# Tree attention on one core: the order of V's loads, GpSimd's copies and the stores, and the first and last loads in other sizes

## The chip, the cores and the metric

The kernel runs on one core of one Trainium2 chip. The metric is the time of one execution on the device in microseconds (us), the median of three runs. A profile of one execution goes with it; the span that it shows is a little shorter than the time, as it begins with the first instruction of the program.

## The reference

Masked attention over 8 batches of 12 heads (96 heads), 512 positions, 64 dimensions, in fp32. The positions are the nodes of a binary tree in heap order, and a node sees itself and its ancestors only:

```python
mask = np.zeros((seq, seq))
for i in range(seq):
    mask[i, i] = 1
    parent = i
    while parent > 0:
        parent = (parent - 1) // 2
        mask[i, parent] = 1
scores = np.einsum('bhqd,bhkd->bhqk', Q, K) * scale      # scale = 1/sqrt(64)
scores = scores + (1 - mask) * (-1e9)
weights = np.exp(scores - np.max(scores, axis=-1, keepdims=True))
weights = weights / (np.sum(weights, axis=-1, keepdims=True) + 1e-10)
return np.einsum('bhqk,bhkd->bhqd', weights, V).astype(np.float32)
```

One head of Q, K, V or the output is 512 x 64 x 4 bytes, 131 KB.

## The kernel before

Heads are loaded in twelve groups of eight ("octets", o = 0 to 11), computed in 48 pairs (i = 0 to 47) and stored in 24 groups of four ("quads", q = 0 to 23). Partition p holds the four nodes 4p to 4p+3, so partitions 0 to 31 hold the nodes under 128 (the top of the tree), 32 to 63 those of level 7 and 64 to 127 the leaves. All loads go through GpSimd's DMA queue, because they cast fp32 to bf16 on the way:

```python
loads = ctx.enter_context(tc.tile_pool(name="loads", bufs=4))
vloads = ctx.enter_context(tc.tile_pool(name="vloads", bufs=4))
opool = ctx.enter_context(tc.tile_pool(name="opool", bufs=15))
NV = 4
...
def load(kept, name, pool, src, o, h0=0, n=8, rows=(0, 128)):
    if o not in kept:
        kept[o] = pool.tile([P, 8, 4, D], bf16, name=name)
    nc.gpsimd.dma_start(
        out=kept[o][rows[0]:rows[1], h0:h0 + n, :, :].rearrange("p h t d -> p h (t d)"),
        in_=src[rows[0]:rows[1], 8 * o + h0:8 * o + h0 + n, :],
    )
```

V has to be spread into the tile `vt`, from which TensorE reads it beside columns of ones. Four DMAs bring an octet of V; two of them go straight into `vt`. GpSimd copies the top rows to four places, VectorE the rest:

```python
def load_v_tiles(o):
    load_v(o, 0, 8, (64, 128))
    for half in range(2):
        nc.gpsimd.dma_start(
            out=vts[o % NV][32 * half:32 * half + 32, :, VCOL[1]:VCOL[1] + 2 * D],
            in_=Vr[32:64, 8 * o:8 * o + 8, 2 * D * half:2 * D * half + 2 * D],
        )
    load_v(o, 0, 8, (0, 32))

def spread_top(o, h0=0, h1=8):
    for j in range(4):
        nc.gpsimd.tensor_copy(
            out=vts[o % NV][32 * j:32 * j + 32, h0:h1, VTOP:VTOP + D],
            in_=vsts[o][0:32, h0:h1, UNITS[TOP + j][1], :],
        )

def spread_leaves(o, upper, h0=0, h1=8):
    nc.vector.tensor_copy(
        out=tile_pair(o, 64 if upper else 0, h0, h1, upper),
        in_=vsts[o][64:128, h0:h1, upper:3 + upper:2, :],
    )
```

The program of GpSimd, in its order. A `yield` only sets where in the program's text the next piece is put; the engine runs its own instructions one after the other:

```python
BEHIND = 8
AHEAD = 3
NO = NQ // 2                       # 12

def pool_program():
    for h0 in (0, 2):
        load_k(0, h0, 2)
        load_q(0, h0, 2)
    load_v(0, 0, 4)
    load_k(0, 4, 4)
    load_q(0, 4, 4)
    load_v(0, 4, 4)
    load_k(1, 0, 4)
    load_q(1, 0, 4)
    spread_top(0, 0, 4)
    load_v_tiles(1)
    load_k(1, 4, 4)
    load_q(1, 4, 4)
    spread_top(0, 4, 8)
    yield
    yield
    for o in range(2, NO):
        load_k(o)
        load_q(o)
        load_v_tiles(o)
        spread_top(o - 1)
        yield
        for q in (2 * o - BEHIND, 2 * o + 1 - BEHIND):
            if q >= 0:
                store(nc.gpsimd, q)
    for q in range(NQ - BEHIND, NQ - 1):
        yield
        store(nc.gpsimd, q)
        if q == NQ - BEHIND + AHEAD:
            spread_top(NO - 1)
```

The main loop; `transpose` and `evac` bring K and Q of a pair into the form for the scores, `values` multiplies by V, `norm` divides and writes the output tile `of`. The last quad goes out through the queues of SyncE and ScalarE:

```python
for i in range(NP + 1):            # NP = 48
    if i < NP:
        scores1(i)
        scores2(i)
    ...
    if i >= 1:
        values(i - 1)
        norm(i - 1)
    for n in (1 if i == 0 else i + 2,):
        if n < NP:
            transpose(n)
            evac(n)
    ...
    spread_vector(i)
    ...                            # the next piece of pool_program
    if i == NP - 1:
        store(nc.sync, NQ - 1, 0, 2)
store(nc.sync, NQ - 1, 2, 1)
store(nc.scalar, NQ - 1, 3, 1)
```

In the profile, line 183 is `load`, 201 the two DMAs straight into `vt`, 209 `spread_top`, 223 `spread_leaves`, 259 `transpose`, 285 `evac`, 346 `values`, 375 the last step of `norm` and 383 `store`.

Of the kernel before, what the change touches and what calls it, by code (L numbers as in the profile page):

```python
# [34 lines left out]
VCOL = (164, 32, 230, 96)  # L35
# [72 lines left out]
def kernel(  # L108
# [7 lines left out]
    nc = tc.nc  # L116
    B, H, S, D = Q.shape
# [3 lines left out]
    NQ = B * H // 4  # L121
# [9 lines left out]
    Vr = V.rearrange("b h (p t) d -> p (b h) (t d)", t=4)  # L131
# [31 lines left out]
    NV = 4  # L163
    NE = 3
    vts, e2s = [], []
# [13 lines left out]
# [9 lines that stand above are left out]
    def load_k(o, h0=0, n=8):  # L188
        load(ksts, "kst", loads, Kr, o, h0, n)

    def load_q(o, h0=0, n=8):
        load(qsts, "qst", loads, Qr, o, h0, n)

    def load_v(o, *args):
        load(vsts, "vst", vloads, Vr, o, *args)

    def load_v_tiles(o):

        load_v(o, 0, 8, (64, 128))
        for half in range(2):  # L200
            nc.gpsimd.dma_start(  # L201
                out=vts[o % NV][32 * half:32 * half + 32, :, VCOL[1]:VCOL[1] + 2 * D],
                in_=Vr[32:64, 8 * o:8 * o + 8, 2 * D * half:2 * D * half + 2 * D],
            )
        load_v(o, 0, 8, (0, 32))

    def spread_top(o, h0=0, h1=8):
        for j in range(4):
            nc.gpsimd.tensor_copy(  # L209
                out=vts[o % NV][32 * j:32 * j + 32, h0:h1, VTOP:VTOP + D],  # L210
                in_=vsts[o][0:32, h0:h1, UNITS[TOP + j][1], :],
            )

    def tile_pair(o, p, h0, h1, first):

        c, step = VCOL[first], VCOL[first + 2] - VCOL[first]
        return vts[o % NV][p:p + 64, h0:h1, c:c + 2 * step].rearrange(
            "p h (t d) -> p h t d", t=2
        )[:, :, :, 0:D]
# [8 lines that stand above are left out]
    def swapped(src, step):  # L228

        return bass.AP(  # L230
            src.tensor, src.offset, [list(src.ap[0]), list(src.ap[1]), [step, 2], [1, D]]
        )

    def spread_l7(o):

        nc.vector.tensor_copy(  # L236
            out=tile_pair(o, 64, 0, 8, 0),
            in_=swapped(vts[o % NV][0:64, :, VCOL[3]:VCOL[3] + D], -D),
        )

    def spread_l7_natural(o, quad, h0, h1):
# [140 lines left out]
    def store(eng, q, h0=0, n=4):  # L382
        eng.dma_start(  # L383
            out=Or[:, 4 * q + h0:4 * q + h0 + n, :],
            in_=ofs[q][:, h0:h0 + n, :, :].rearrange("p h t d -> p h (t d)"),
        )


    BEHIND = 8

    AHEAD = 3
    NO = NQ // 2

    def pool_program():

        for h0 in (0, 2):
            load_k(0, h0, 2)
            load_q(0, h0, 2)
        load_v(0, 0, 4)
        load_k(0, 4, 4)  # L400
        load_q(0, 4, 4)
        load_v(0, 4, 4)
        load_k(1, 0, 4)
        load_q(1, 0, 4)
        spread_top(0, 0, 4)
        load_v_tiles(1)
        load_k(1, 4, 4)
        load_q(1, 4, 4)
        spread_top(0, 4, 8)
        yield  # L410
        yield
        for o in range(2, NO):
            load_k(o)
            load_q(o)
            load_v_tiles(o)
            spread_top(o - 1)
            yield
            for q in (2 * o - BEHIND, 2 * o + 1 - BEHIND):
                if q >= 0:
                    store(nc.gpsimd, q)  # L420
        for q in range(NQ - BEHIND, NQ - 1):
            yield
            store(nc.gpsimd, q)
            if q == NQ - BEHIND + AHEAD:
                spread_top(NO - 1)

    def spread_first(quad, parts):

        for part in parts:
            if part < 4:  # L430
                spread_l7_natural(0, part, 4 * quad, 4 * quad + 4)
            else:
                spread_leaves(0, part - 4, 4 * quad, 4 * quad + 4)

    def spread_vector(i):

        if i == 1 or i == 2:
            spread_first(1, range(3) if i == 1 else range(3, 6))
        o, step = divmod(i + 2, 4)
        if 1 <= o < NO:  # L440
            if step == 0:
                spread_leaves(o, 0)
            elif step == 1:
                spread_leaves(o, 1)
                spread_l7(o)

    def pool_until(done, wanted):
        while done < wanted:
            next(program, None)
            done += 1  # L450
        return done

    program = pool_program()
    steps = pool_until(0, 1)
    transpose(0)
    evac(0)
    for i in range(NP + 1):
# [3 lines that stand above are left out]
        if i == 1:  # L461
            transpose(2)
            evac(2)
            spread_first(0, range(4, 6))
# [7 lines that stand above are left out]
        if i == 0:  # L472
            spread_first(0, range(4))
        spread_vector(i)
        if steps < NO:
            steps = pool_until(steps, min((i + 11) // 4, NO))
        else:
            steps = pool_until(steps, min(steps + 2, NO + (i - 2) // 2 - (NQ - 1 - BEHIND)))
        if i == NP - 1:
            store(nc.sync, NQ - 1, 0, 2)  # L480
# [32 lines left out]
```

The softmax here doesn't subtract the row's maximum and nothing guards it: scores larger than these inputs give would overflow.

## Time and profile before

| | us |
|---|---|
| time, median of 3 runs (lowest, highest) | 140.59 (140.56, 141.06) |
| span in the profile | 138.3 |
| PE (TensorE matmul) busy | 107.7 |
| GpSimd busy | 102.1 |
| VectorE busy | 96.5 |
| ScalarE busy | 84.3 |
| HBM read, written | 38.21 MB, 12.58 MB |

Busy time says how long an engine had an instruction in work, not whether anything waited for it. The strips of the page cut the span into 40 slices of 3.46 us, one digit a slice, in tenths. A line of a timeline gives start, length, engine, line of the kernel, operation, what it writes and reads, how often, and in brackets the idle time before it and what ended it. A DMA that GpSimd issues has two times: the issue, which occupies GpSimd, and the landing, some us later, when its bytes are there.

### The profile page before, as it was taken

Reading aid. Unit: us, or ns where it says so; the run is one execution under the profiler, and the core shown is the slowest. Engines: PE = TensorE matmul, PEld = TensorE weight load, DVE = VectorE, ACT = ScalarE, POOL = GpSimd, SP = SyncE. Lnnn points to the kernel's source line nnn. Section 1 sums busy time; section 2 is a strip of 40 time slices with the busy share of each in tenths; the row PEclk is TensorE's granted clock in tenths of the full one; section 3 lists DMA queues with packets and bytes.
Section 4 is the critical chain, followed back from the end, with each engine's and each line's share of the span. In section 5 each row is a group of like instructions: output and inputs, shape, how many; then the busy total and the mean of one; then the engine's idle time right before and its main releaser. Section 6 shows DMA issues by size and latency. Waiting matters only on the chain.

```text
span 138.3 us, 5482 instructions
## 1 busy us (share of the span) xinstructions
PE 107.7 (78%) x2400; PEld 78.6 (57%) x2400; DVE 96.5 (70%) x205; ACT 84.3 (61%) x98; POOL 102.1 (74%) x155
## 2 busy tenths in 40 slices
PE   0486798799879996968998995795895894997920
PEld 0243566577656774746676674574574583675610
DVE  4036688889788698759698884684784775788550
ACT  4044075768775866848686774595595486486810
POOL 6969999749599896797598399489489489489200
PEclk9999689999999999999999999999999999999985
DMA  4999999999999999999999999999999999999982
GB/s 137 155 136 189 195 192 197 198 191 198 192 198 194 335 220 195 323 227 197 295 254 196 280 272 194 257 291 198 244 303 198 229 315 202 221 366 390 364 302 92
DMA packets 44936, 32.27 MB, mean 233 GB/s; under 512 B 7280, under 2 KB 41840, under 8 KB 44912
## 3 DMA queue, kind: packets, MB, share of 16 engines
q0 software_dynamic: 44208, 30.94, 127.2%
q1 hardware_dynamic: 560, 0.85, 1.8%
q8 instruction: 18, 0.29, 0.8%
q10 hardware_dynamic: 144, 0.13, 0.3%
q14 instruction: 6, 0.05, 0.1%
HBM read 38.21 MB, written 12.58 MB: 367 GB/s over the span
## 4 chain that ended last, share of the span: by engine, by line
PE 34%; DMA 27%; DVE 16%; POOL 9%; issue 9%; ACT 1%; POOLq 0%; ACTq 0%
DMA qst<-in_Q_dram 27%; PE ob L346 15%; PE kqp L259 8%; DVE of L375 5%; PE s L296 4%; POOL vt L209 3%; DVE vt L223 3%; DVE kq L285 3%; PE s L301 3%; DVE vt L236 3%; PE s L325 3%; PE s L318 2%; DVE rec L372 2%; POOL kst L183 2%; POOL out_dram L383 1%
## 5 line engine op out<-in xcount | busy, mean ns | idle before, releaser
L307 ACT ACTIVATE e<-s 128x1024 bf16<-128x1024 f32 x48 | 49.1, 1023 | 46.8 <-PE s L301 46.1
L346 PE MATMUL ob<-vt,e 128*128 128x65 bf16 (+1 forms) x960 | 39.3, 198 | 14.3 <-POOL vt L209 7.1
L346 PEld LDWEIGHTS <-e 128*128 128x128 bf16 (+1 forms) x960 | 31.3, 103 | 20.8 <-issue 9.3
L285 DVE COPY kq<-kqp 128x1024 bf16<-128x1024 bf16 x48 | 32.8, 683 | 9.5 <-PE kqp L259 9.4
L331 ACT ACTIVATE e<-s 128x768 bf16<-128x768 f32 x48 | 38.6, 805 | 0.0
L375 DVE TENSOR_TENSOR of<-ob,rec 128x512 f32<-128x512 f32 x48 | 33.2, 692 | 1.9 <-DMA out_dram<-of 0.2
L209 POOL COPY vt<-vst 32x512 bf16<-32x512 bf16 (+1 forms) x52 | 31.1, 598 | 3.5 <-DMA vst<-in_V_dram 1.3
L372 DVE RECIPROCAL rec<-ob 128x8 f32<-128x8 f32 x48 | 9.9, 207 | 23.7 <-PE ob L346 23.2
L259 PE MATMUL kqp<-ctile,qst 128*64 128x128 bf16 x384 | 20.1, 226 | 5.3 <-DMA qst<-in_Q_dram 3.2
L259 PE MATMUL kqp<-ctile,kst 128*64 128x128 bf16 x384 | 19.7, 225 | 5.2 <-DMA kst<-in_K_dram 5.2
L183 POOL DMA_DIRECT2D qst<-in_Q_dram x15 | 12.7, 849 | 11.7 <-PE kqp L259 6.6
L383 POOL DMA_DIRECT2D out_dram<-of x23 | 17.6, 768 | 5.0 <-DVE of L375 4.7
L325 PEld LDWEIGHTS <-kq 64*128 64x128 bf16 x384 | 15.9, 97 | 7.1 <-issue 1.6
L296 PE MATMUL s<-ctile 64*128 64x512 bf16 x96 | 19.4, 400 | 0.1
L301 PE MATMUL s<-kq 64*128 64x512 bf16 x96 | 18.9, 391 | 0.5 <-DVE kq L285 0.5
L183 POOL DMA_DIRECT2D vst<-in_V_dram x24 | 16.2, 676 | 2.4 <-DMA vt<-in_V_dram 2.4
L325 PE MATMUL s<-kq 64*128 64x96 bf16 (+3 forms) x384 | 17.9, 213 | 0.1
L259 PEld LDWEIGHTS <-qst 128*64 128x64 bf16 x384 | 14.0, 114 | 5.4 <-DMA qst<-in_Q_dram 4.3
L318 PE MATMUL s<-ctile 64*128 64x384 bf16 x96 | 16.2, 334 | 0.2
L259 PEld LDWEIGHTS <-kst 128*64 128x64 bf16 x384 | 12.9, 114 | 5.4 <-DMA kst<-in_K_dram 5.2
L201 POOL DMA_DIRECT2D vt<-in_V_dram x22 | 12.7, 585 | 4.1 <-DMA qst<-in_Q_dram 2.2
L183 POOL DMA_DIRECT2D kst<-in_K_dram x15 | 13.0, 868 | 2.2 <-POOLq L497 0.8
(15 smaller groups left out, 42.3 us busy)
## 6 DMA issues: line engine op xcount, KB each, us to landing
out_dram<-of POOLq DMA_DIRECT2D x23, 512.0 KB, 8.2
kst<-in_K_dram POOLq DMA_DIRECT2D x10, 512.0 KB, 10.0
qst<-in_Q_dram POOLq DMA_DIRECT2D x10, 512.0 KB, 10.1
vst<-in_V_dram POOLq DMA_DIRECT2D x13, 256.0 KB, 10.1
vt<-in_V_dram POOLq DMA_DIRECT2D x22, 64.0 KB, 9.7
vst<-in_V_dram POOLq DMA_DIRECT2D x11, 128.0 KB, 9.7
kst<-in_K_dram POOLq DMA_DIRECT2D x3, 256.0 KB, 7.2
qst<-in_Q_dram POOLq DMA_DIRECT2D x3, 256.0 KB, 7.6
```

The costliest lines, as they stand in the source:

```text
L183: nc.gpsimd.dma_start(out=kept[o][rows[0]:rows[1], h0:h0 + n, :, :].rearrange("p h t d -> p h (t d)"), in_=src[rows[0]:rows[1], 8 * o + h0 ...
L209: nc.gpsimd.tensor_copy(out=vts[o % NV][32 * j:32 * j + 32, h0:h1, VTOP:VTOP + D], in_=vsts[o][0:32, h0:h1, UNITS[TOP + j][1], :],)
L259: nc.tensor.transpose(out=dst, in_=st[i // 4][:, 2 * (i % 4) + a, t, :], identity=perm)
L285: nc.vector.tensor_copy(out=kq[:, :, :, :].rearrange("p k (x y) c -> p k x (y c)", x=2), in_=src)
L296: nc.tensor.matmul(out=sp[:, a, :], lhsT=k1code[64 * a:64 * a + 64, :], rhs=q1code[64 * a:64 * a + 64, :], start=True, stop=False,)
L301: nc.tensor.matmul(out=sp[:, a, :], lhsT=keys(i, a, TOP), rhs=qTs[i][64 * a:64 * a + 64, :, :].rearrange("p t c -> p (t c)"), start=False, ...
L307: nc.scalar.activation(out=et[:, :, :, :].rearrange("p a t c -> p (a t c)"), in_=sp[:, :, :].rearrange("p a c -> p (a c)"), func=AF.Exp, s ...
L325: nc.tensor.matmul(out=sp[:, a, :, :].rearrange("p t c -> p (t c)")[:, lo:hi], lhsT=keys(i, a, TILE2[tile2]), rhs=qTs[i][64 * a:64 * a + 6 ...
L331: nc.scalar.activation(out=e2s[i % NE][:, :, :, 32:128].rearrange("p a t c -> p (a t) c"), in_=sp[:, :, :, 32:128].rearrange("p a t c -> p ...
L346: nc.tensor.matmul(out=ob[lo:hi, a, start_o:start_o + 65], lhsT=e[:, a, QPOS[t], lo:hi], rhs=vt[:, 2 * (i % 4) + a, col:col + 65], **flags,)
L375: nc.vector.tensor_tensor(out=ofs[q][:, 2 * r:2 * r + 2, :, :], in0=vals, in1=rec[:, :, :, :].to_broadcast([P, 2, 4, D]), op=ALU.mult,)
L383: eng.dma_start(out=Or[:, 4 * q + h0:4 * q + h0 + n, :], in_=ofs[q][:, h0:h0 + n, :, :].rearrange("p h t d -> p h (t d)"),)
```

## The change

Four things at once. (1) V's nodes under 128 are loaded first of V's four DMAs, not last, and GpSimd's copies of the octet before stand between the loads of Q and V, not behind V's. This is to have the copies done sooner after their rows have landed. (2) Stores go ten quads behind the computation, not eight: the loads get two stores fewer ahead of them, and the end two more. (3) The last octet is loaded and spread in two halves of four heads, so that its first half can be used before its second has come. (4) The first K and Q come as one load of four heads each, not two of two.

```diff
-    def load_v_tiles(o):
-
-        load_v(o, 0, 8, (64, 128))
+    def load_v_tiles(o, h0=0, n=8):
+
+        load_v(o, h0, n, (0, 32))
+        load_v(o, h0, n, (64, 128))
         for half in range(2):
             nc.gpsimd.dma_start(
-                out=vts[o % NV][32 * half:32 * half + 32, :, VCOL[1]:VCOL[1] + 2 * D],
-                in_=Vr[32:64, 8 * o:8 * o + 8, 2 * D * half:2 * D * half + 2 * D],
+                out=vts[o % NV][32 * half:32 * half + 32, h0:h0 + n, VCOL[1]:VCOL[1] + 2 * D],
+                in_=Vr[32:64, 8 * o + h0:8 * o + h0 + n, 2 * D * half:2 * D * half + 2 * D],
             )
-        load_v(o, 0, 8, (0, 32))
...
-    BEHIND = 8
-
-    AHEAD = 3
+    BEHIND = 10
     NO = NQ // 2
 
     def pool_program():
 
-        for h0 in (0, 2):
-            load_k(0, h0, 2)
-            load_q(0, h0, 2)
+        load_k(0, 0, 4)
+        load_q(0, 0, 4)
         load_v(0, 0, 4)
...
+        behind = (1, 0, 8)
         for o in range(2, NO):
-            load_k(o)
-            load_q(o)
-            load_v_tiles(o)
-            spread_top(o - 1)
+            for h0, n in ((0, 8),) if o < NO - 1 else ((0, 4), (4, 4)):
+                load_k(o, h0, n)
+                load_q(o, h0, n)
+                spread_top(nc.gpsimd, *behind)
+                load_v_tiles(o, h0, n)
+                behind = (o, h0, h0 + n)
             yield
             for q in (2 * o - BEHIND, 2 * o + 1 - BEHIND):
                 if q >= 0:
                     store(nc.gpsimd, q)
+        spread_top(nc.gpsimd, *behind)
         for q in range(NQ - BEHIND, NQ - 1):
             yield
             store(nc.gpsimd, q)
-            if q == NQ - BEHIND + AHEAD:
-                spread_top(NO - 1)
...
-        if 1 <= o < NO:
+        if 1 <= o < NO - 1:
             if step == 0:
                 spread_leaves(o, 0)
             elif step == 1:
                 spread_leaves(o, 1)
                 spread_l7(o)
+        elif i + 1 in (4 * NO - 4, 4 * NO - 2):
+
+            h0 = i + 5 - 4 * NO
+            spread_leaves(NO - 1, 0, 2 * h0, 2 * h0 + 4)
+            spread_leaves(NO - 1, 1, 2 * h0, 2 * h0 + 4)
+            spread_l7(NO - 1, 2 * h0, 2 * h0 + 4)
```

(`spread_l7` and `spread_top` take the range of heads as arguments for it, and `spread_top` the engine, which is GpSimd everywhere.)

More of the change, by code (lines that the diff above doesn't have):

```diff
@@ L195, in load_v, with spread_top @@
         load(vsts, "vst", vloads, Vr, o, *args)
-    def load_v_tiles(o):
-        load_v(o, 0, 8, (64, 128))
+    def load_v_tiles(o, h0=0, n=8):
+        load_v(o, h0, n, (0, 32))
+        load_v(o, h0, n, (64, 128))
         for half in range(2):
             nc.gpsimd.dma_start(
-                out=vts[o % NV][32 * half:32 * half + 32, :, VCOL[1]:VCOL[1] + 2 * D],
-                in_=Vr[32:64, 8 * o:8 * o + 8, 2 * D * half:2 * D * half + 2 * D],
-            )
-        load_v(o, 0, 8, (0, 32))
-    def spread_top(o, h0=0, h1=8):
+                out=vts[o % NV][32 * half:32 * half + 32, h0:h0 + n, VCOL[1]:VCOL[1] + 2 * D],
+                in_=Vr[32:64, 8 * o + h0:8 * o + h0 + n, 2 * D * half:2 * D * half + 2 * D],
+            )
+    def spread_top(eng, o, h0, h1):
         for j in range(4):
-            nc.gpsimd.tensor_copy(
+            eng.tensor_copy(
                 out=vts[o % NV][32 * j:32 * j + 32, h0:h1, VTOP:VTOP + D],
@@ L232, in swapped, with spread_l7 @@
         )
-    def spread_l7(o):
+    def spread_l7(o, h0=0, h1=8):
         nc.vector.tensor_copy(
-            out=tile_pair(o, 64, 0, 8, 0),
-            in_=swapped(vts[o % NV][0:64, :, VCOL[3]:VCOL[3] + D], -D),
+            out=tile_pair(o, 64, h0, h1, 0),
+            in_=swapped(vts[o % NV][0:64, h0:h1, VCOL[3]:VCOL[3] + D], -D),
         )
@@ L404, in pool_program @@
         load_q(1, 0, 4)
-        spread_top(0, 0, 4)
+        spread_top(nc.gpsimd, 0, 0, 4)
         load_v_tiles(1)
@@ L408, in pool_program @@
         load_q(1, 4, 4)
-        spread_top(0, 4, 8)
+        spread_top(nc.gpsimd, 0, 4, 8)
         yield
         yield
+        behind = (1, 0, 8)
         for o in range(2, NO):
-            load_k(o)
-            load_q(o)
-            load_v_tiles(o)
-            spread_top(o - 1)
+            for h0, n in ((0, 8),) if o < NO - 1 else ((0, 4), (4, 4)):
[4 more added lines that the diff above has]
+                behind = (o, h0, h0 + n)
             yield
```

## The prediction

> **What bounds the kernel now.** I read the page's strips of the span first, because the busy shares alone (PE 78%, POOL 74%, DVE 70%) name no bound.
>
> ```profile
> DMA  4999999999999999999999999999999999999982
> GB/s 137 155 136 189 195 192 197 198 191 198 192 198 194 335 220 195 323 227 197 295 254 196 280 272 194 257 291 198 244 303 198 229 315 202 221 366 390 364 302 92
> ```
>
> The DMA digit is 9 in every slice but the first and the last two. The GB/s strip must be read with the cast in mind: a load reads fp32 from HBM and writes bf16, and the page counts what was written, so 198 in a slice of loads is 396 GB/s of HBM reads; a slice of stores alone shows 390. Both are the same speed. To put a number on it I asked for sums over stretches (columns: stretch, then the engines' busy time with counts, clock, DMA share, GB/s).
>
> ```profile
> 0.00:4.00 4.00, 0.00 (x0) 0.00 (x0) 1.39 (x16) 1.49 (x2) 2.94 (x8) 1.00 0.54 141
> 4.00:8.00 4.00, 2.41 (x22) 1.19 (x24) 0.69 (x1) 0.00 (x0) 4.00 (x7) 1.00 1.21 148
> 8.00:12.00 4.00, 3.69 (x50) 2.09 (x44) 2.17 (x5) 2.59 (x3) 2.57 (x6) 1.00 1.26 155
> 12.00:16.00 4.00, 2.12 (x40) 1.75 (x42) 1.74 (x6) 0.87 (x2) 3.96 (x7) 0.83 1.45 196
> 122.00:126.00 4.00, 3.73 (x91) 2.74 (x88) 3.54 (x8) 3.31 (x5) 3.71 (x6) 1.00 1.06 397
> 130.00:132.00 2.00, 1.28 (x31) 0.98 (x29) 0.84 (x3) 1.79 (x3) 0.75 (x1) 1.00 0.84 320
> 132.00:134.00 2.00, 0.78 (x20) 0.64 (x20) 1.00 (x3) 0.00 (x0) 0.00 (x0) 1.00 0.98 360
> 134.00:136.00 2.00, 0.00 (x0) 0.00 (x0) 0.25 (x1) 0.00 (x0) 0.00 (x0) 0.52 0.65 225
> ```
>
> 122 to 126 is nothing but stores: 397 GB/s, which I take as full rate. The page gives 38.21 MB read and 12.58 MB written; 50.79 MB at 397 GB/s is 127.9 us. The span is 138.3, so all there is to win is 10.4 us, and I place it. In 0 to 4 us 564 KB were moved, of which 459 KB are the constants and 105 KB loads (210 KB of HBM): 1.7 us of work, 2.3 lost. 4 to 8 (148, so 296 of HBM): 1.0 lost. 8 to 12 (310): 0.9. From 12 on 196, full. In the tail: 130 to 132 lose 0.4, 132 to 134 0.2, 134 to 136 0.9, the last 2.3 us nearly all of themselves. With 0.2 for 126 to 130 (377 and 375 GB/s) that is 3.9. What is left, about 2.3, is spread over 100 us in the middle.
>
> Then the chain of waits, in order of time, to see whether the middle is bandwidth or latency:
>
> ```profile
> 77.88 10.59 DMA qst<-in_Q_dram
> 88.47 0.04 issue
> 88.52 0.43 PE kqp L259 x8
> ...
> 89.03 10.06 DMA qst<-in_Q_dram
> 99.10 0.04 issue
> 99.14 0.43 PE kqp L259 x8
> ...
> 99.67 9.97 DMA qst<-in_Q_dram
> ```
>
> Each Q load takes 10 us from issue to landing, is used at once, and the next one is issued 0.55 us after it landed. In the trace's semaphore records GpSimd's DMAs signal on eight semaphores in turn, so each waits for the landing of the one eight before; an octet of heads (K, Q, four of V, two stores) is eight DMAs. The loop looks like latency but is bandwidth: an octet is 24 heads of loads and 8 of stores at 131 KB, 4.19 MB, 10.57 us at 397 GB/s, and the period here is 10.6.
>
> Last, GpSimd in order of time, where the change works:
>
> ```profile
> 89.03 0.88 POOL L183 DMA_DIRECT2D qst<-in_Q_dram  x1 [1.77 <-PE kqp L259]
> 90.31 0.69 POOL L183 DMA_DIRECT2D vst<-in_V_dram  x1 [0.40 <-DMA vt<-in_V_dram]
> 90.99 1.16 POOL L201 DMA_DIRECT2D vt<-in_V_dram  x2
> 92.13 0.60 POOL L183 DMA_DIRECT2D vst<-in_V_dram  x1
> 92.77 2.67 POOL L209 COPY vt<-vst 32x512 bf16<-32x512 bf16 x4
> ```
>
> Four copies, 2.67 us, end at 95.44; PE starts the first product of that octet at 95.49. Its Q landed at 88.47, so the copies are 7 us behind it.
>
> **What the skill says.** The Trainium skill, "DMA: Bandwidth & Descriptors", section Specifications, gives about 358 GB/s as HBM's limit per core and 435 as the fabric's. This trace shows 397 for whole stretches; the measurement decides and I use 397. "Perfetto Trace Analysis", section DMA Optimizations, says both that larger DMAs fill the bandwidth better and that splitting lets work start sooner when the engines are idle. Here they are not idle before the tail, and the fixed part is visible: a 2-head load needs 3.9 us to landing (list of DMA issues: 128 KB, 3.9) for 0.66 us of bytes. "SBUF — State Buffer", on the shared port pair, says that some VectorE copies and any GpSimd work exclude each other. It agrees: the leaf copies of L223 take 0.42 us at 69.86 and 0.81 at 71.93, beside the GpSimd copies.
>
> **The change, part by part.**
>
> Start: before, four issues of two heads (K, Q, K, Q, 0.72 us apart) go ahead of V, each 0.66 us of bytes, so GpSimd hands out work a little slower than it is moved. After, two issues of four heads (about 0.8 us each, like the four-head ones that follow) hand out 1.32 us of bytes each. I take 0.3 us of the 1.0 lost in 4 to 8. The 0.9 lost in 8 to 12 stays: all ten first loads had been issued by 8.7 and the rate was still 155, so issue is not its cause. The first transposes start about 1 us later, which is hidden: values of pair 0 wait until 13 us for the second half of Q anyway.
>
> Copies between Q and V: with V's top 32 rows first, they land 0.66 us after Q, and the copies run from 0.55+0.88 = 1.4 to 4.1 us after Q instead of to 7.0. PE's first product then waits for its own chain: from the octet's first transposes (68.08) to its first product (74.60) it is 6.5 us. So the octet gains about 0.5 to 0.9 us of lag, off the path. The new V loads go out 2.7 us later, at 4.1 us after Q; what is still queued then (rest of V, two stores, K, Q) lasts to 10.6 us after Q, so DMA does not run dry. Worth: 0.
>
> Stores ten behind: the same bytes. Two stores of 524 KB, 2.64 us, move from before the last load to after it. The last load landed at 123.0; now near 120.3. Twelve stores instead of ten follow, 15.8 us. By itself 0, but compute finishes earlier against DMA.
>
> Last heads by fours: before, compute set the end. The last copies wait in GpSimd's order behind stores, run from 123.66 to 126.42, then four pairs of products to 133.3, the last output at 134.25, and the last two stores, issued at 134.3, land 3 us later. After, the last Q lands near 119; 6.5 us to product 46 and 2.1 to product 47, with 1 us for the output: near 129. The stores last to 136. Compute leaves the path, and of the 1.5 us lost from 130 to 136 I give back 1.0.
>
> The price: GpSimd runs in order and the last octet has twelve small loads instead of six. From the landing of Q of octet 10: Q11a out at 0.55 (0.81 us), four copies (2.65), four V DMAs (2.35), K and Q (1.62): GpSimd reaches the copies of 11a at 7.98. Their V rows land at 8.3 (V10 2.65, two stores 2.65, K and Q 2.65, 0.33). Copies of four heads took 1.69 us (at 10.03), so the next V load goes out at 10.0. From issue to the first bytes I take the issue's length plus 1.07 us (first load: issued 1.27 to 2.09, its first packet in the trace at 3.18). The queued work ends at 11.9; the four small V DMAs, issued 0.57 to 0.62 us apart, hold 1.32 us of bytes and end at 13.6; the next store, out at 12.3, can move at 14.2: idle 0.3 + 0.6. Then the last copies (1.7 us) hold up the third store: idle 0.55. Sum 1.45; some lies under the engines that lag, so 1.2.
>
> Sum: -0.3 (start) -1.0 (old tail) +1.2 (new gap near 120) = -0.1 us. The timed 140.59 becomes about **140.5 us**.
>
> **The rivals.** (1) The gap does not appear, because the bytes start sooner after the issue than I take: then -1.3, 139.3. For it: the only cold measurement of that delay is the first load. (2) The gap is paid in full and the twelve stores at the end also suffer from engines that finish unevenly (128 to 130 shows 375 with GpSimd idle and stores queued): +0.5 to +1.3, 141.1 to 141.9. (3) Earlier V tops shorten every octet, because PE waits 7.1 us in total for L209: some 5 us, 135. Against it: DMA shows 9 throughout, and an octet already takes its byte time. (4) Late V loads starve DMA in each octet: 7 octets of about 1 us, 147; against it stand the 6 us still queued.
>
> **Range and chances.** Terms of -1.3 and +1.3 around a sum near 0 give 139.2 to 142.0 for 8 in 10. Two per cent is 2.8 us: faster needs nearly all the lost time of start and tail, slower needs two new gaps. Faster 0.05, same 0.89, slower 0.06.
>
> **What would show it.** Right: DMA digits of 9 up to 115 us; PE's wait for L209 nearly gone; last products before 130; a dip in GB/s near 118 to 122; stores at 390 to the end. Wrong: octets of Q loads much off 10.6 us, or no dip and an end before 136.5 in the span.

## The result, and the profile after

| | before | changed |
|---|---|---|
| time, median | 140.81 us | 144.75 us |
| lowest to highest of the runs | 140.56 to 141.06 | 144.5 to 145.55 |
| span in the profile | 138.3 us | 142.5 us |

The ratio is 1.029, 95% interval 1.024 to 1.034: slower by some 2.9%, above the range of 139.2 to 142.0. (The first line has four runs of each kernel.)

First the strips of the page, of the changed kernel:

```profile
DMA  4999999999999999999999999999999999999991
GB/s 132 150 187 196 192 196 198 194 195 197 193 197 191 199 209 333 204 205 332 198 209 334 200 212 326 203 213 325 202 216 324 169 168 212 305 312 324 338 326 43
```

The digit strip says nothing new: 9 almost to the end. The GB/s strip does. The third and fourth slices are better than before (187 and 196 against 136 and 189). From 110 to 118 us there are two slices of 169 and 168, and then the stores alone run at 305 to 338, where the kernel before had 366, 390 and 364.

Sums over stretches put numbers on it (columns: stretch and length, busy time and count of PE, PEld, DVE, ACT, POOL, clock, DMA share, GB/s). The changed kernel:

```profile
4.00:8.00 4.00, 0.64 (x9) 0.40 (x10) 0.00 (x0) 0.00 (x0) 3.37 (x5) 1.00 1.32 170
8.00:12.00 4.00, 3.75 (x40) 2.10 (x40) 0.93 (x2) 1.72 (x2) 2.36 (x6) 1.00 1.41 189
112.00:116.00 4.00, 3.72 (x84) 2.74 (x85) 3.71 (x7) 2.60 (x4) 3.43 (x8) 1.00 1.31 162
116.00:120.00 4.00, 4.00 (x100) 3.05 (x99) 2.99 (x6) 3.32 (x5) 3.96 (x8) 1.00 1.21 166
124.00:128.00 4.00, 3.49 (x76) 2.52 (x78) 3.45 (x10) 2.98 (x5) 3.61 (x5) 1.00 0.97 305
132.00:136.00 4.00, 0.00 (x0) 0.00 (x0) 0.62 (x1) 0.00 (x0) 0.00 (x0) 0.50 1.01 341
```

The kernel before, in three of these stretches:

```profile
112.00:116.00 4.00, 3.13 (x72) 2.23 (x67) 3.63 (x7) 3.32 (x5) 3.87 (x7) 1.00 1.31 258
116.00:120.00 4.00, 3.07 (x78) 2.34 (x77) 1.71 (x4) 1.86 (x3) 3.03 (x5) 1.00 1.49 199
124.00:128.00 4.00, 3.26 (x83) 2.48 (x81) 3.44 (x7) 2.86 (x4) 3.74 (x6) 1.00 1.00 387
```

Before, 124 to 128 was 387 GB/s at a DMA share of 1.00. Here it is 305 at 0.97, and 341 at 1.01 from 132 to 136, when compute is over and GpSimd's stores have long been issued. So from 124 to 136 us the DMA engines are not idle: they are busy and move less. The packets say the same. A store packet of 4 KB took 165 ns (median) from 123 to 132 us before, and 187 to 198 ns (medians of stretches of 2 us) from 120 to 138 us in the changed kernel.

The whole difference, as time lost against 397 GB/s (bytes of the trace's packets in each stretch, without the fetches of instructions, a load counted at its fp32 size; good to about 0.1), up to the last packet:

```
us lost in          before   changed   difference
0 to 12               4.27      3.50     -0.8
12 to 112             2.16      2.41     +0.25
112 to 120            0.09      1.94     +1.85
120 to last packet    2.50      4.18     +1.7
sum                   9.02     12.03     +3.0
```

The last packet ends at 136.96 before and 139.96 after, 3.0 us later. The remaining 1.2 us of the span lie behind it. A drain stands at the end of GpSimd's program; in the trace it ends at 137.31 before, 1.3 us behind GpSimd's last landing (136.03), and at 141.69 after, 1.6 us behind it (140.13). Before, this was hidden behind the stores of SyncE and ScalarE, the last of which landed at 137.34; now GpSimd's last store is the last to land but for one (140.35).

GpSimd in order of time, changed kernel, where the middle rows of the table come from:

```profile
107.01 0.75 POOL L183 DMA_DIRECT2D qst<-in_Q_dram  x1 [2.13 <-DMA qst<-in_Q_dram]
107.81 2.55 POOL L209 COPY vt<-vst 32x512 bf16<-32x512 bf16 x4
110.31 1.17 POOL L183 DMA_DIRECT2D vst<-in_V_dram  x2
111.46 1.10 POOL L202 DMA_DIRECT2D vt<-in_V_dram  x2
112.54 0.78 POOL L183 DMA_DIRECT2D kst<-in_K_dram  x1
113.28 0.78 POOL L183 DMA_DIRECT2D qst<-in_Q_dram  x1
114.50 1.70 POOL L209 COPY vt<-vst 32x256 bf16<-32x256 bf16 x4 [0.44 <-DMA vst<-in_V_dram]
116.15 1.17 POOL L183 DMA_DIRECT2D vst<-in_V_dram  x2
117.30 1.09 POOL L202 DMA_DIRECT2D vt<-in_V_dram  x2
118.38 1.53 POOL L383 DMA_DIRECT2D out_dram<-of  x2
119.95 1.70 POOL L209 COPY vt<-vst 32x256 bf16<-32x256 bf16 x4
121.60 6.00 POOL L383 DMA_DIRECT2D out_dram<-of  x8
```

From the issue of the Q load at 107.01 to that of the next load at 110.31 it is 3.3 us, 2.55 of them copies, and there are two such pauses more (113.28 to 116.15, 119.14 to 121.60). After 121.60 the stores are issued 0.75 us apart, far faster than they are moved: from there nothing in GpSimd's order can slow them.

One more reading is needed for what follows. A DMA is done by 16 engines, and each reports its own end to the semaphore, so the trace has 16 ends for each DMA. "First" and "last" below are the first and the last of them; what a store takes is the step from one store's end to the next one's.

```
                        issued   first end (step)   last end (step)
before,   Q of octet 11  110.21   117.09             120.24
          store of q 16  118.31   123.76 (1.29)      127.48 (1.29)
          store of q 18  122.12   126.50             131.04
          store of q 19  122.87   127.81 (1.31)      132.14 (1.10)
          store of q 20  126.37   129.69 (1.88)      133.44 (1.30)
          store of q 21  127.11   131.26 (1.57)      134.72 (1.28)
changed,  Q11, 1st half  107.01   111.13             114.11
          V top rows     110.31   112.33             114.45
          store of q 17  123.84   129.58 (1.52)      131.17 (1.64)
          store of q 18  124.58   131.13 (1.55)      132.85 (1.68)
          store of q 19  125.33   132.69 (1.56)      134.41 (1.56)
```

Before, the leading engine runs 3 us ahead of the last one at the end of the loads. In the changed kernel it is through with the Q load at 111.1, while the next load was issued only at 110.31: it has nothing to do until about 112 (an estimate: the first end of V's top rows, less 0.33 us for their bytes). By the second half of Q the engines lie 1.1 us apart (117.50 and 118.62), and the leading one then takes 1.5 to 1.7 us for nearly every store, where 1.3 was usual.

### The profile page after: what moved, and what is told of

The parts are those of the page before. It is cut to its first block, busy times and chain, and to the rows that moved or that the text cites. A ratio compares the mean times of both kernels' runs of the same rounds, so it can differ in the third digit from the quotient of the medians.

```text
span 142.5 us, 5490 instructions
## 1 busy us (share of the span) xinstructions
PE 108.2 (76%) x2400; PEld 79.5 (56%) x2400; DVE 95.9 (67%) x208; ACT 84.4 (59%) x98; POOL 104.0 (73%) x163
## 4 chain that ended last, share of the span: by engine, by line
DMA 27%; PE 25%; POOL 24%; issue 9%; DVE 7%; POOLq 0%
DMA vst<-in_V_dram 13%; POOL vt L209 11%; PE ob L346 10%; DMA vt<-in_V_dram 7%; DMA qst<-in_Q_dram 7%; PE kqp L259 5%; PE s L296 3%; POOL vst L183 3%; POOL vt L202 3%; DVE of L375 3%; POOL qst L183 3%; POOL kst L183 3%; PE s L301 2%; PE s L325 2%; PE s L318 2%
## 5 line engine op out<-in xcount | busy, mean ns | idle before, releaser
L346 PE MATMUL ob<-vt,e 128*128 128x65 bf16 (+1 forms) x960 | 40.2, 199 | 9.6 <-DVE of L375 4.4
L259 PE MATMUL kqp<-ctile,qst 128*64 128x128 bf16 x384 | 20.6, 227 | 4.2 <-issue 3.5
L259 PEld LDWEIGHTS <-qst 128*64 128x64 bf16 x384 | 14.6, 115 | 4.1 <-issue 3.2
L183 POOL DMA_DIRECT2D vst<-in_V_dram x26 | 16.7, 648 | 0.0
L202 POOL DMA_DIRECT2D vt<-in_V_dram x24 | 14.0, 591 | 0.0
```

Source lines behind the costliest of these rows:

```text
L183: nc.gpsimd.dma_start(out=kept[o][rows[0]:rows[1], h0:h0 + n, :, :].rearrange("p h t d -> p h (t d)"), in_=src[rows[0]:rows[1], 8 * o + h0 ...
L259: nc.tensor.transpose(out=dst, in_=st[i // 4][:, 2 * (i % 4) + a, t, :], identity=perm)
L346: nc.tensor.matmul(out=ob[lo:hi, a, start_o:start_o + 65], lhsT=e[:, a, QPOS[t], lo:hi], rhs=vt[:, 2 * (i % 4) + a, col:col + 65], **flags,)
```

## The experiments

Each run stands beside runs of the kernel before on the same chip; ratios are to those, with 95% intervals. The results first:

| run | what it is | us | ratio |
|---|---|---|---|
| changed | all four parts | 144.75 | 1.029 (1.024 to 1.034) |
| e1_whole | changed, last octet whole | 142.55 | 1.014 (1.004 to 1.025) |
| e3_before_behind10 | before, stores ten behind | 140.99 | 1.002 (0.999 to 1.005) |
| e4_skew | changed, uneven loads ahead of the last stores | 146.58 | 1.043 (1.035 to 1.051) |
| e5_sync | before, stores held until the last V has landed | 150.14 | 1.064 (1.054 to 1.074) |
| e6_level_not_dry | e5_sync and a load ahead of the stores | 149.95 | 1.065 (1.058 to 1.073) |
| e10_load_among | e5_sync and a load among the stores | 152.2 | 1.081 (1.071 to 1.090) |
| e9_fours_late | changed, last copies moved back | 142.52 | 1.015 (1.012 to 1.018) |
| e7_whole_late | changed, last octet whole, last copies moved back | 139.13 | 0.988 (0.981 to 0.995) |
| e8_before_first4 | before, first K and Q by fours | 138.94 | 0.988 (0.979 to 0.997) |
| e11_whole_late8 | e7_whole_late, stores eight behind | 139.78 | 0.996 (0.993 to 0.999) |

**Which theory of the long store steps.** Three stood at first: that engines at the same point slow each other (LEVEL), that a long run of stores is slow by itself (TWELVE), and that only the pauses count (GAP).

*e1_whole*, the last octet as the others:

```diff
-            for h0, n in ((0, 8),) if o < NO - 1 else ((0, 4), (4, 4)):
+            for h0, n in ((0, 8),):
```

> The changed kernel with the last octet loaded and spread whole, as the other octets are (no loads by fours at the end); all else as changed. Three theories for the slow end of the changed kernel (stores of 512 KB land 1.55 to 1.6 us apart from 122 us on, against 1.3 before). LEVEL: the gaps between the small last loads let all 16 DMA engines come level (from the first to the last engine's completion of one DMA 1.1 us there, 3.7 us before), and level engines store more slowly. Without the small loads there is no gap, the engines keep their spread of about 3 us, twelve stores land 1.3 us apart: 139.5 to 140.5 us. TWELVE: a long run of stores with no loads between is slow by itself; twelve stores still land about 1.6 us apart: 143 to 144 us. GAP: only the idle time of the small loads counts, about 2 us of it: 142.5 us, with stores unchanged at 1.6 us apart.

Measured 142.55, the number that GAP gave, but not for its reason. The small loads are gone, and the trace shows a pause all the same, and a longer one: GpSimd's last copies now stand behind only two stores and wait for V's top rows.

```profile
113.22 1.55 POOL L383 DMA_DIRECT2D out_dram<-of  x2
118.56 2.54 POOL L209 COPY vt<-vst 32x512 bf16<-32x512 bf16 x4 [3.80 <-DMA vst<-in_V_dram]
121.05 5.97 POOL L383 DMA_DIRECT2D out_dram<-of  x8
```

The two stores ahead of the copies took 1.30 us (first and last engine alike); those behind took the leading engine 1.5 to 1.6 from the first one on. That was the pattern to follow.

*e3_before_behind10*, one constant of the kernel before:

```diff
-    BEHIND = 8
+    BEHIND = 10
```

> The kernel before with stores ten groups behind and nothing else changed. LEVEL: no small loads, no gap, the engines keep their spread of 3 us or more, the twelve stores at the end land 1.3 us apart, time 140 to 141 us as before. TWELVE: two more stores in the run at the end make it slower: stores about 1.5 us apart on average, 142 to 143.5 us. GAP: no gap, time as before, 140.5 to 141.

140.99, no difference: ten behind costs nothing by itself. The steps were not as any theory had them. Six of the stores took about 1.29 us. GpSimd's other five, issued behind the last copies, took the leading engine 1.5 to 1.9, while the spread of the engines was 2.6 us before the copies and still 2.1 to 2.5 behind them. TWELVE doesn't explain the jump, and LEVEL doesn't fit well.

*e4_skew* puts the engines out of step. The added loads are extra work that no output needs:

```diff
+            if o == NO - 1:
+                for n, heads in ((0, 16), (1, 32), (2, 48)):
+                    nc.gpsimd.dma_start(
+                        out=spare[4 * n:4 * n + 4, 0:heads, :], in_=Qr[4 * n:4 * n + 4, 0:heads, :],
+                    )
             yield
```

> The changed kernel with three loads added behind the last load of V, of four partitions and 16, 32 and 48 heads each, into a tile that nothing reads. Each occupies only some of the DMA engines, for about 0.65, 1.3 and 2 us, so that the engines go into the run of stores at different points. They add 393 KB, 1.0 us of the mean engine and 2 us of the most loaded. LEVEL: the stores then land about 1.3 to 1.4 us apart, packets of 4 KB take 165 to 170 ns against 190 to 206 in the changed kernel; the time falls or stays although bytes are added, 141.5 to 144.5 us. TWELVE: stores stay 1.55 to 1.6 us apart, and the added bytes make it 145.5 to 147 us. GAP: same as TWELVE.

146.58. The engines went into the stores 4.4 us apart, and still the first end went on in steps of 1.72, 1.63, 1.57 and 1.54 us, while the last end, that of the engines with the largest added load, went on in steps of 1.29, 1.28, 1.30 and 1.34. At the same time, on the same stores, some engines took long steps and some short ones. So it belongs to the single engine, not to the HBM as a whole. From 121 to 122 us, ahead of the first store, only 8 to 12 of the 16 engines had a packet under way. Read with the ends, the engines with long steps had come to the end of their queue by then, and those with short steps still had a load in work; the trace doesn't name the engines, so this is argued here and tested in the next runs.

*e5_sync* makes all engines run empty in the kernel before:

```diff
             spread_top(o - 1)
+            if o == NO - 1:
+                spread_top(NO - 1)
             yield
...
-            if q == NQ - BEHIND + AHEAD:
-                spread_top(NO - 1)
```

> The kernel before with GpSimd's last four copies moved ahead of the stores of the last octet, so that no store goes out until the last of V has landed: the DMA engines run dry for some 4 us and start level into ten stores. Nothing of the last octet is loaded in small pieces. LEVEL: the ten stores land about 1.6 us apart, 3 us more than 1.3 apart, and the time is 140.6 + 4 + 3, 147 to 148.5 us. TWELVE and GAP: the idle time alone is added and the stores land 1.3 us apart as before, 144 to 145.5 us.

150.14, more than expected, as the pause was longer (the queue is empty from 124 to 128). The long steps came out: nine stores, no step of the leading engine under 1.52 us, without a small load anywhere. LEVEL and an after-effect of an empty queue (DRY) both explain it; the next run parts them.

*e6_level_not_dry*, e5_sync with one added load, into a tile that nothing reads:

```diff
             if o == NO - 1:
                 spread_top(NO - 1)
+                nc.gpsimd.dma_start(out=spare[:, :, :], in_=Qr[:, 0:8, :])
             yield
```

> The kernel of the run e5_sync (no store until the last of V has landed) with one more load of eight heads behind the wait and ahead of the stores, into a tile that nothing reads. The DMA engines start level into that load, but have it in work (2.65 us) when the first store reaches them, so none of them stands idle between the last load and the first store. LEVEL (engines at the same point store slowly): stores still land 1.55 us apart; 150.1 + 2.65, about 152.5 to 153.5 us. DRY (an engine whose queue runs empty ahead of the stores moves them slowly from then on, one that goes over from loads without a pause moves them at full rate): stores land 1.3 us apart, packets of 4 KB take 165 ns instead of 190; 149.5 to 150.5 us in spite of the added load.

149.95 us: a megabyte more to read, and the same time within the spread of the runs (the spans of the two profiles are 146.9 and 148.5). The engines were level (0.8 us from first to last), and the first stores took 1.28, 1.29 and 1.30 us. The stretch of stores, first in e5_sync, then in e6_level_not_dry:

```profile
130.00:134.00 4.00, 2.69 (x62) 1.94 (x56) 1.80 (x4) 2.61 (x4) 3.36 (x5) 1.00 1.00 313
134.00:138.00 4.00, 0.10 (x6) 0.00 (x0) 0.90 (x2) 0.00 (x0) 0.00 (x0) 0.89 1.01 328
```

```profile
134.00:138.00 4.00, 0.78 (x20) 0.64 (x20) 1.11 (x3) 0.00 (x0) 1.49 (x2) 0.78 1.03 408
138.00:142.00 4.00, 0.00 (x0) 0.00 (x0) 0.00 (x0) 0.00 (x0) 0.00 (x0) 0.50 1.02 371
142.00:146.00 4.00, 0.00 (x0) 0.00 (x0) 0.00 (x0) 0.00 (x0) 0.00 (x0) 0.50 1.03 371
```

The share is 1.0 in both; the rate is 313 to 328 against 408. LEVEL falls: level engines can store at full rate. For the first stores it counts whether an engine meets them with an empty queue or coming from a load.

That is one way into the long steps and not the only one. From 138 on the rate in e6_level_not_dry is 371, and from 144 to 146 the median packet of 4 KB takes 189 ns. GpSimd had issued seven stores by 133.0, and no engine stood idle from 134 to 145 (16 packets under way throughout). SyncE's store came in at 138, but e10_load_among, below, has SyncE's stores too and keeps its rate. In e3_before_behind10 as well the share of 4-KB packets of up to 170 ns falls from 0.55 (127 to 129 us) to 0.15 (132 to 134), again with about 16 packets under way. What ends the full rate there is not shown.

*e10_load_among* asks what ends the long steps (`spare` is again a tile that nothing reads):

```diff
             store(nc.gpsimd, q)
+            if q == NQ - BEHIND + 1:
+                nc.gpsimd.dma_start(out=spare[:, :, :], in_=Qr[:, 0:8, :])
```

> The kernel of the run e5_sync (DMA engines empty for some 4 us, then stores, which land 1.55 us apart) with one load of eight heads into an unread tile behind the fourth of the stores. DRY, with a state that a load ends: the stores ahead of the load land 1.55 us apart, those behind it 1.3; about 151 us (150.1 + 2.65 - 6 x 0.27). DRY, with a state that lasts until the end whatever comes: 1.55 on both sides, 152.8 us. A limit of stores in a row without loads, whatever went before: 1.3 just behind the load, rising later.

152.2 lies between the expectations, since the stores of SyncE came among GpSimd's (ends from 142.2 to 146.2) and stretch the steps there. The undisturbed steps decide: 1.62 and 1.60 us ahead of the load, 1.29 and 1.29 at the end behind it. In stretches, ahead and behind:

```profile
130.00:133.00 3.00, 1.86 (x34) 1.18 (x33) 1.77 (x4) 2.40 (x3) 3.00 (x5) 1.00 1.01 317
145.00:146.00 1.00, 0.00 (x0) 0.00 (x0) 0.00 (x0) 0.00 (x0) 0.00 (x0) 0.50 1.03 399
```

A load ends them; nine stores in a row, in e5_sync, don't.

**Which part of the change.**

*e9_fours_late* keeps the small loads and moves the copies back:

```diff
-                spread_top(nc.gpsimd, *behind)
+                if h0 == 0:
+                    spread_top(nc.gpsimd, *behind)
...
-        spread_top(nc.gpsimd, *behind)
         for q in range(NQ - BEHIND, NQ - 1):
             yield
             store(nc.gpsimd, q)
+            if q == NQ - BEHIND:
+                spread_top(nc.gpsimd, NO - 1, 0, 4)
+            elif q == NQ - BEHIND + 2:
+                spread_top(nc.gpsimd, NO - 1, 4, 8)
```

> The changed kernel with the last octet still in fours, but GpSimd's last copies moved behind the loads and behind three and five of the stores, so that they no longer hold up loads. If the small loads are slow by themselves: 142 to 143 us. If only the waits of GpSimd that let the queue run empty count: 139.3 to 140.8 us, GB/s near 390 of HBM all the way to 126 us.

142.52, the number of the case in which the small loads cost by themselves. One reason is in the trace (two lines of GpSimd's timeline and one stretch):

```profile
110.58 1.17 POOL L183 DMA_DIRECT2D vst<-in_V_dram  x2
111.73 1.10 POOL L202 DMA_DIRECT2D vt<-in_V_dram  x2
112.00:116.00 4.00, 3.99 (x95) 3.02 (x96) 3.16 (x8) 2.77 (x4) 4.00 (x7) 1.00 1.16 145
```

The four V loads of half an octet take GpSimd 2.2 us to issue and hold 1.32 us of bytes (524 KB at 397 GB/s). GpSimd was busy in all of 112 to 116, with no wait, and the rate was 145 GB/s. The copies for octet 10 stood ahead of these loads still. That is not all of the cost: the first four stores took 1.36 to 1.43 us, the later ones 1.5 to 1.7, with two pauses of their own for copies (119.05 to 120.69, 122.23 to 123.87). The run doesn't part the two.

*e7_whole_late* takes both away:

```diff
-            for h0, n in ((0, 8),) if o < NO - 1 else ((0, 4), (4, 4)):
+            for h0, n in ((0, 8),):
...
-        spread_top(nc.gpsimd, *behind)
         for q in range(NQ - BEHIND, NQ - 1):
             yield
             store(nc.gpsimd, q)
+            if q == NQ - BEHIND + 1:
+                spread_top(nc.gpsimd, *behind)
```

> The run e1_whole (changed kernel, last octet whole) with GpSimd's last copies behind four of the twelve stores at the end and not behind two, so that the queue is not empty when they wait. LEVEL and DRY alike: no gap near 122 us, stores 1.3 us apart for most of the tail, and the better start (about 1.1 us) is kept: 139 to 140.3 us. If a run of twelve stores is slow by itself: 142 us as e1_whole.

139.13, 1.2% under the kernel before, with ten behind and the new order still in it. Stretches of its tail:

```profile
120.00:124.00 4.00, 4.00 (x101) 2.94 (x96) 3.32 (x8) 3.45 (x4) 4.00 (x6) 1.00 1.00 381
124.00:128.00 4.00, 3.46 (x82) 2.61 (x81) 3.34 (x8) 2.86 (x4) 0.88 (x2) 1.00 1.02 366
```

Even here the leading engine went over to long steps (first end in steps of 1.5 us from 125.4 on), but the last one kept 1.29 us to 133.6, and the last one sets the end.

*e8_before_first4*, the kernel before with the first loads alone:

```diff
-        for h0 in (0, 2):
-            load_k(0, h0, 2)
-            load_q(0, h0, 2)
+        load_k(0, 0, 4)
+        load_q(0, 0, 4)
```

> The kernel before with the first K and Q as one load of four heads each. If the start of the changed kernel (less lost by 12 us: 3.5 us of full rate against 4.3) comes from this part alone, 139.6 to 140.0 us; if it comes from the order of V's rows or is lost again, 140.5 to 141.

138.94, a little better than expected. The stretches say where:

```profile
4.00:8.00 4.00, 0.53 (x8) 0.40 (x8) 0.00 (x0) 0.00 (x0) 3.36 (x5) 1.00 1.27 167
8.00:12.00 4.00, 3.05 (x35) 1.72 (x35) 0.69 (x1) 1.12 (x2) 1.71 (x5) 1.00 1.44 194
```

8 to 12 had been 155 with loads of two heads. This part of the change is the good one. Up to 12 us it loses 3.4 us of full rate, where the kernel before lost 4.3; the span is 1.4 us shorter, so some 0.5 of the gain lies elsewhere and is not explained.

*e11_whole_late8*, e7_whole_late with `BEHIND = 8`:

> The run e7_whole_late with the stores eight groups behind, so that of the changed kernel only the order of V and the copies and the first loads by fours are left. As no engine runs empty before the last stores, 138.7 to 139.5 us, the same as e7_whole_late (139.1) and e8_before_first4 (138.9): then the number of groups behind and the order of the copies are worth nothing here and the first loads are worth all of it. If the order of V is worth something by itself: 138.0 to 138.5.

139.78, above what was expected, and 0.4% under the kernel before in 22 runs, its interval overlapping those of e7_whole_late and e8_before_first4. The order of V and the copies shows no gain of its own. The best of all runs are e8_before_first4 and e7_whole_late, not to be told apart.

## Why the prediction was wrong, point by point

**What bounds the kernel**: right. DMA is the bound, and an octet takes its byte time: the lost time from 12 to 112 us differs by 0.25 us in 100.

**Start, -0.3**: direction right, size wrong: -0.8. The step that failed is "The 0.9 lost in 8 to 12 stays". That all ten first loads had been issued by 8.7 was true, but the rate there depended on their size: with loads of four heads the same stretch lost 0.2 (189 GB/s where 155 had been). That the engines run empty between two-head loads would fit, and is only argued.

**Copies between Q and V, worth 0**: no run shows a gain or a loss from them away from the end, and PE's wait for the copies (7.1 us before) is gone from the list of waits. In its place GpSimd waits for V:

```profile
POOL vt L209 <- DMA vst<-in_V_dram: 8.2, 5, 3.4
```

That wait was not in the prediction. In the middle it cost nothing; at the end, in e1_whole, it is the pause.

**Stores ten behind, 0 by itself**: right (e3_before_behind10, 1.002).

**Compute leaves the path, -1.0**: it did leave it, though later than predicted: the last output is ready at 132.6 (near 129 in the prediction), and the last store lands at 140.3. Nothing came back, because the stores themselves became slower, and because GpSimd's own end, 1.2 us, came out from behind the stores of the other queues.

**The gap near 120, +1.2**: there, and +1.85 in the table. The step that failed is "The queued work ends at 11.9", counted from the landing of Q. A landing is the end of the last of 16 engines, and the leading one was 3 us ahead. So the gap opened earlier than worked out, already behind the copies for octet 10 (at 111.1, where 11.9 us behind Q of octet 10 is 118.3), and "some lies under the engines that lag, so 1.2" went the wrong way: the lag hides from the landing that the engines ahead have run empty. A third term erred the other way. The 1.07 us from the end of an issue to the first bytes, taken from the first load, was 0.57 in e5_sync, with all engines empty (issue over at 127.39, first packet at 127.96).

**"Stores at 390 to the end"**: this is the step that failed most, and a cost that the sum left out. The changed kernel's engines, having run empty, moved the stores at 305 to 341 GB/s, the leading one in 1.5 to 1.7 us each and not 1.3. An estimate: twelve stores at about 0.27 us more are 3.2 us, of the 4.18 lost behind 120; the tail before lost 2.50 there, in part waiting for compute, and the net is the +1.7 of the table. The rival that named uneven engines, read off 375 GB/s from 128 to 130, had the right view in hand and the wrong reading. In the kernel before, too, up to 3 of the 16 engines stood idle from 127.5 to 128 us, ahead of q 20 (step 1.88, then 1.57), and the leading one took long steps from there.

Rivals (3) and (4) of the prediction are out: the octets are neither shorter nor starved (the leading engine ends Q of octets 8, 9 and 10 at 81.99, 92.58 and 103.18, 10.6 us apart).

## What to carry to other kernels

Where DMA is the bound, count what is still queued from the leading engine's end and not from the landing, and keep work in the queue through every pause of the engine that issues, above all where loads give way to stores. Small transfers are dear where their issue takes longer than their bytes (2.2 us for 1.32 here). A change of several parts may hide a good one: here the two lines of the start were worth about 0.8 us of lost time (1.2%, with an interval of 0.3 to 2.1%, in the one run that has them alone), and the rest took it back and 2.9% on top.

## What was not expected of the hardware

A DMA engine that meets a store with an empty queue moves this store and the following ones at about 0.83 of its rate (in e5_sync some 1.56 us a store against 1.29; a 4-KB packet in 192 ns against 165), with the queue full behind it, through all of the nine stores of e5_sync (128 to 145 us). On the same stores other engines, which came over from earlier work without a pause, keep the full rate (last end in steps of 1.28 to 1.34 us in e4_skew and e7_whole_late), some of them for a few stores only. One load of 1 MB brings the rate back (e6_level_not_dry, e10_load_among), even where it is useless work. An engine can also come into the long steps without an idle moment (e6_level_not_dry from 138 on). Why an engine is so is open; the runs show an empty queue as enough for it, not the cause.

Also, GpSimd's drain ends 0.4 to 1.6 us behind the landing of its last DMA (1.3 before, 1.6 in the changed kernel, 0.4 in e6_level_not_dry), so where GpSimd's stores land last, this stands at the end of the span.
